# A third Strassen-type pair in the gate/up projection, and two groups of PSUM banks that change places

## The chip, the cores and the metric

The kernel runs on one core of a Trainium2 chip. The core has a matrix engine (TensorE, PE in the profile, with its weight loads as PEld), three engines for elementwise work (VectorE or DVE, ScalarE or ACT, GpSimd or POOL) and SyncE (SP), which issues most of the loads here. Matmuls write to PSUM, eight banks of 128 x 512 fp32 values; everything else lies in SBUF. The metric is the time of one execution on the device, in microseconds (us), the median of several runs.

## What is computed

One decoder layer on 256 tokens of width 2048, in fp32. The change touches the feed-forward part alone:

```python
ff = silu(u @ w_ffn_gate) * (u @ w_ffn_up)    # u: 256 x 2048, weights 2048 x 5632
h = h + ff @ w_ffn_down                       # 5632 x 2048
return rmsnorm(h, final_norm_w)
```

Ahead of it stand an input projection, a recurrent unit (RG-LRU), a retention unit with eight heads, and an output projection added to the residual `h`; `u` is the normalised `h`.

## The kernel before

**Products in three matmuls.** Every fp32 operand is split in two parts, a rounded high one and the rest as a low one. ScalarE casts the high part (line 101) and VectorE subtracts it from the operand (line 102). A product of a left block (128 x 128, the stationary operand) and a right block (128 x 512, the moving one) is then three matmuls: high by high, high by low, low by high (lines 667 to 669). All three add up in one PSUM bank.

**Quads.** Gate/up runs as 11 blocks (`NB`), each for 512 columns of gate and the same 512 of up. A block goes through eight quads. A quad covers 256 of the 2048 input features: the left side is a 2 x 2 arrangement of 128 x 128 blocks `a11` to `a22` (rows are the two halves of the tokens, columns the two halves of the features), and the right side a 2 x 2 arrangement of 128 x 512 blocks `b11` to `b22` (rows are the halves of the features, column 1 is gate, column 2 is up). The four outputs are `c11`, `c21` (gate, two halves of the tokens) and `c12`, `c22` (up).

**Eight or seven products.** A plain quad takes the eight products of `EIGHT`. A quad whose number is in `SUMMED` takes the seven of `SEVEN`, a Strassen-Winograd scheme: the right side needs the sums `t1` to `t4` (lines 628 to 632, VectorE), the left side the sums `s1` to `s4` (lines 532 to 535, made once for a pair, in the output projection before). Four of the seven products, `p1`, `p5`, `p6`, `p7`, are shared: they add up over all summed quads of a block in four banks of their own, and are read after the last one and combined into starting values of the outputs (`post`, lines 723 to 732). Before the change `SUMMED` holds 2 and 4. The down projection has its own list, `SUMMED_DOWN`, and uses the same `block` function.

**What a quad loads and cuts.** `Quad.load` is called for each half of a quad: one transfer of 512 KB into a slot of the pool `raw` (five slots of 128 x 1024), issued by SP (line 614). A plain quad splits each half into one slot each of `wh` and `wl` (pool `split`, four slots of either). A summed quad splits `b11` by itself, makes the sums in two further slots of `raw`, and then splits `t1` with `t2`, `t3` with `t4` and `b22` with `b21`, three slots of `wh` and `wl`.

**PSUM.** Two pools of four banks: `bank` (pool `pmm`) and `aux` (pool `paux`). In gate/up and down, the outputs `c11` to `c22` take `aux` and the shared products `p1` to `p7` take `bank` (line 663). `bank` also serves the transposes of the gated product (`turn`, lines 714 to 721), those of the residual in blocks 1 and 2 (`resid_tok`, line 579) and the two small matmuls of the norm (`norm2`, line 568).

**The end of a block.** With `c12` and `c22` complete, `post` adds the shared part (lines 733 to 736), and `gated` applies tanh on ScalarE and two multiplications on VectorE (lines 708 to 712). `turn(0)` and `turn(1)` transpose the result for the down projection, and ScalarE copies it out (line 721). They are put off with `defer(n, ...)`, which runs a function n program steps later; a step is one quad. `turn(0)` is put off by 2 and `turn(1)` by 3: behind the first and the second quad of the next block.

**Who sets the order.** The program is traced step by step, with loads three half-quads ahead. The order of each engine's instructions is then settled at build time by a planner, which goes by data, free slots and modelled durations, with earlier traced work first (`schedule_with_timeline_sim=True`, line 1060). So matmuls of a later product can stand ahead of earlier ones. On the chip each engine runs its list in order and waits where an operand or a slot isn't there. Only the end of the last down block is ordered by hand (line 683).

Of the kernel before, what the change touches and what calls it, by code (L numbers as in the profile page):

```python
# [28 lines left out]

SUMMED = (2, 4)
SUMMED_DOWN = (2, 5, 8, 11, 14)


# [1 line left out]
def tile_hymba_layer(ctx: ExitStack, tc: tile.TileContext, A: dict, out: bass.AP):  # L37
# [17 lines left out]
    def nm(s):  # L55
        counter[0] += 1
        return f"{s}_{counter[0]}"

    def act_tile(name, dt=F32):
        return apool.tile([P, 512], dt, tag="act", name=nm(name))  # L60
# [7 lines left out]
    def bank(name):  # L68
        return pmm.tile([P, 512], F32, tag="mm", name=nm(name))
# [10 lines left out]
    def xs(k):  # L80
        return xt[k // 2][:, (k % 2) * S : (k % 2) * S + S]
# [137 lines left out]
    def defer(steps, f):  # L219
        later.append([steps, f])  # L220
# [12 lines left out]
    def rsqrt_small(dst, var, scale, n):  # L233

        t0 = cpool.tile([P, n], F32, name=nm("rs0"))
        t1 = cpool.tile([P, n], F32, name=nm("rs1"))
        act.activation(out=t1, in_=var, func=AF.Sqrt, scale=scale, bias=eps_t)
        v.tensor_scalar(out=t0, in0=var, scalar1=scale, scalar2=EPS, op0=ALU.mult, op1=ALU.add)
        v.reciprocal(out=t1, in_=t1)

        v.tensor_tensor(out=t0, in0=t0, in1=t1, op=ALU.mult)
        v.tensor_tensor(out=t0, in0=t0, in1=t1, op=ALU.mult)
        v.tensor_scalar(out=t0, in0=t0, scalar1=-0.5, scalar2=1.5, op0=ALU.mult, op1=ALU.add)
        v.tensor_tensor(out=dst, in0=t0, in1=t1, op=ALU.mult)
# [300 lines left out]
    def out_post(f, ps):  # L545
# [10 lines left out]
        if f % 2:  # L556
            hh[f // 2] = Left(hf[0], f // 2 in SUMMED)
        sq = sumsq[:, :S] if f == 0 else act_tile("sq")[:, :S]
# [6 lines left out]

    def norm2():

        ps = bank("rms")
        for t in range(2):
            pe.matmul(ps[:, 2 * t : 2 * t + 2], sumsq[:, t * P : t * P + P], ones[:, 0:2], start=True, stop=True)  # L570
        rsqrt_small(r2_tok, ps[:, 0:4:2], 1.0 / D, 2)
        v.tensor_scalar(out=r2_half, in0=r2_tok, scalar1=0.5, scalar2=None, op0=ALU.mult)
        v.tensor_tensor(out=r2_sq, in0=r2_half, in1=r2_tok, op=ALU.mult)
# [2 lines left out]

    def resid_tok(cb):
        for t in range(2):
            ps = bank("ht")
            for i in range(4):  # L580
                pe.transpose(ps[:, i * P : i * P + P], xs(4 * cb + i)[:, t * P : t * P + P], ident)
            htok[(cb, t)] = xpool.tile([P, 512], F32, tag="xh", name=nm("htok"))
            act.copy(out=htok[(cb, t)], in_=ps)

# [5 lines left out]
    class Quad:  # L592
# [19 lines left out]
        def load(self, half):  # L612
# [20 lines left out]
            self.cut(("t3", "t4"), tb)  # L633
            self.cut(("b22", "b21"), r)

    EIGHT = (
        ("c11", "a11", "b11"), ("c11", "a12", "b21"), ("c21", "a21", "b11"), ("c21", "a22", "b21"),
        ("c12", "a11", "b12"), ("c12", "a12", "b22"), ("c22", "a21", "b12"), ("c22", "a22", "b22"),
# [6 lines left out]
    def block(quads, lefts, post, ps, tail=(), after=None, ordered=False):  # L645


        n = len(quads) - (2 if tail else 0)
        todo = [(i, c, a, b, 0, 512) for i, q in enumerate(quads[:n]) for c, a, b in (SEVEN if q.sums else EIGHT)]
        for c, c0, cw in tail:  # L650
            todo += [(n, c, a, b, c0, cw, i) for i in range(n, len(quads)) for o, a, b in EIGHT if o == c[:3]]
        firsts, lasts = {}, {}
        for m, (_, c, *_) in enumerate(todo):
            firsts.setdefault(c, m)
            lasts[c] = m
        at = [0]

        def step(i):
            def run():
                while at[0] < len(todo) and todo[at[0]][0] == i:  # L660
                    m, (_, c, a, b, c0, cw, *q) = at[0], todo[at[0]]
                    if firsts[c] == m:
                        ps[c] = (aux if c in ("c11", "c12", "c21", "c22") else bank)(c)
                    q = q[0] if q else i
                    (ah, al), (bh, bl) = lefts[q][a], (t[:, c0 : c0 + cw] for t in quads[q].parts[b])
                    p, last = ps[c][:, c0 : c0 + cw], lasts[c] == m
                    pe.matmul(p, ah, bh, start=firsts[c] == m, stop=False)  # L667
                    pe.matmul(p, ah, bl, start=False, stop=False)  # L668
                    pe.matmul(p, al, bh, start=False, stop=last)  # L669
                    if last:  # L670
                        post(c)
                    at[0] += 1
                if after:
                    after(i)

            return run

        for i in range(n):
            program.append(([quads[i]], step(i)))
        if tail:  # L680

            def end():
                with tc.manual_schedule(engines={nc.tensor.engine}) if ordered else ExitStack():
                    step(n)()

            program.append((quads[n:], end))

    def ffn_block(j):
        def after(i):
            if j == 0 and i == SUMMED[-1] + 1:  # L690
                norm2()
            if j in (1, 2) and i < 2:
                resid_tok(2 * j - 2 + i)
            if j == NB - 1 and i == 0:
                load_fw()

        ps = {}
        quads = [Quad(A["w_gu"][j * (KT // 2) + i], i in SUMMED) for i in range(KT // 2)]
        block(quads, hh, ffn_post(j, ps), ps, after=after)

    def ffn_post(j, ps):
        part = {}

        def other(c, name, a, b, op=ALU.subtract):
            part[c] = act_tile(name)
            v.tensor_tensor(out=part[c], in0=a, in1=b, op=op)

        def gated(t):
            g, u, th = part["c21" if t else "c11"], part["c22" if t else "c12"], act_tile("th")
            act.activation(out=th, in_=g, func=AF.Tanh, scale=r2_half[:, t : t + 1])  # L710
            v.scalar_tensor_tensor(out=g, in0=th, scalar=1.0, in1=g, op0=ALU.add, op1=ALU.mult)
            v.scalar_tensor_tensor(out=g, in0=u, scalar=r2_sq[:, t : t + 1], in1=g, op0=ALU.mult, op1=ALU.mult)

        def turn(b):
            pt = bank("ft")
            for c in range(2):
                for t, g in enumerate((part["c11"], part["c21"])):
                    o = c * S + t * P
                    pe.transpose(pt[:, o : o + P], g[:, (2 * b + c) * P : (2 * b + c) * P + P], ident)  # L719
            ff[2 * j + b] = act_tile("ff")  # L720
            act.copy(out=ff[2 * j + b], in_=pt)

        def post(c):
            if c == "p1":
                part["c11"] = act_tile("c11")
                act.copy(out=part["c11"], in_=ps[c])
            elif c == "p7":
                n = act_tile("n")
                v.tensor_tensor(out=n, in0=ps["p6"], in1=part["c11"], op=ALU.subtract)
                other("c12", "c12", n, ps["p5"])  # L730
                other("c21", "c21", n, ps["p7"])
                other("c22", "c22", part["c21"], ps["p5"])
            elif c in ("c11", "c12", "c22"):
                v.tensor_tensor(out=part[c], in0=ps[c], in1=part[c], op=ALU.add)
            elif c == "c21":
                v.tensor_tensor(out=part[c], in0=ps[c], in1=part[c], op=ALU.subtract)
            if c == "c12":
                gated(0)
            if c == "c22":
                gated(1)  # L740
                defer(2, lambda: turn(0))
                defer(3, lambda: turn(1))

        return post

# [3 lines left out]
    def load_fw():  # L749
        for c in range(4):  # L750
            fw[c] = late_tile("fw")
            nc.sync.dma_start(out=fw[c], in_=A["final_norm_w"][c * 512 : c * 512 + 512].partition_broadcast(P))
# [136 lines left out]
    for n in range(NLRU):  # L889

        def post(ps, n=n):
            defer(max(1, 4 - n), lambda: lru_in(n, ps))
            defer(max(9, 12 - n), lambda: lru_gate(n))
            if n == NLRU - 1:
                defer(10, lru_roots)
                for m in range(NLRU):
                    defer((12, 15, 18, 20, 22, 24, 26, 28)[m], lambda m=m: lru_scan(m))
# [54 lines left out]
    for step, (units, run) in enumerate(program):  # L952
        need += 2 * len(units)
        while done < min(len(loads), need + AHEAD):
            un, j = loads[done]
# [108 lines left out]
```

## Time and profile before

| | us |
|---|---|
| runs shown: median (lowest to highest) | 1105.15 (1104.84 to 1106.02) |
| the profiled execution | 1106.04 |
| its span, first to last instruction | 1103.3 |
| gate/up begins | 382.8 |
| gate/up blocks 5 to 10, each | 43.15 |

The granted clock of TensorE is 0.998 on the mean. In the rows of the profile a group is written as line, engine, operation, the tiles it writes and reads (out<-in), its shape and count; then the busy time in us, the mean duration of one in ns, and after the second bar the idle time of the engine just before these instructions, with what ended it. In a table of stretches the first number is the length, and then come each engine's busy time and instructions, the granted clock, the share of the DMA engines and GB/s. In the timeline a row is start, duration, engine, line, what it does, how many in a row were merged, and in brackets the idle time before it and its releaser. Matmul ends are modelled, so their starts are the better measure.

### The profile page before, as it was taken

Reading aid. Unit: us, or ns where it says so; the run is one execution under the profiler, and the core shown is the slowest. Engines: PE = TensorE matmul, PEld = TensorE weight load, DVE = VectorE, ACT = ScalarE, POOL = GpSimd, SP = SyncE. Lnnn points to the kernel's source line nnn. Section 1 sums busy time; section 2 is a strip of 40 time slices with the busy share of each in tenths; the row PEclk is TensorE's granted clock in tenths of the full one; section 3 lists DMA queues with packets and bytes.
Section 4 is the critical chain, followed back from the end, with each engine's and each line's share of the span. In section 5 each row is a group of like instructions: output and inputs, shape, how many; then the busy total and the mean of one; then the engine's idle time right before and its main releaser. Section 6 shows DMA issues by size and latency. Waiting matters only on the chain.

```text
span 1103.3 us, 14624 instructions
## 1 busy us (share of the span) xinstructions
PE 1092.4 (99%) x5328; PEld 920.5 (83%) x5328; DVE 885.3 (80%) x1249; ACT 622.1 (56%) x846; POOL 57.9 (5%) x64
## 2 busy tenths in 40 slices
PE   9999999999999999999999999999999999999996
PEld 7888888888888988888888888888888888888885
DVE  7798799978776787788787878877887999777874
ACT  7666644468665665554554545544545675554552
POOL 0602130000000000000000000000000000020001
PEclk9999999999999999999999999999999999999999
DMA  9765575554665465645746646556456465646562
GB/s 329 239 199 168 171 245 170 176 188 143 194 220 187 155 207 174 213 154 186 247 132 214 226 156 229 187 191 219 159 195 234 153 219 196 224 161 218 201 230 76
DMA packets 62215, 214.71 MB, mean 195 GB/s; under 512 B 7104, under 2 KB 7488, under 8 KB 62144
## 3 DMA queue, kind: packets, MB, share of 16 engines
q1 hardware_dynamic: 61344, 211.70, 57.6%
q0 software_dynamic: 512, 1.57, 0.5%
q8 instruction: 41, 0.67, 0.3%
q10 hardware_dynamic: 288, 0.52, 0.1%
q14 instruction: 30, 0.25, 0.1%
HBM read 211.67 MB, written 2.10 MB: 194 GB/s over the span
## 4 chain that ended last, share of the span: by engine, by line
PE 98%; DVE 0%; DMA 0%; SPq 0%; ACT 0%; issue 0%; DVEq 0%
PE c L667 18%; PE c L669 18%; PE c L668 18%; PE fm L140 16%; PE fm L141 8%; PE p L667 3%; PE p L668 3%; PE p L669 3%; PE tm L156 3%; PE tm L157 3%; PE tm L158 3%; PE ft L719 1%; DMA x<-in_x 0%; PE fm L147 0%; PE fm L145 0%; PE fm L146 0%
## 5 line engine op out<-in xcount | busy, mean ns | idle before, releaser
L102 DVE TENSOR_TENSOR wl<-raw,wh 128x1024 fp32r<-128x1024 f32 (+1 forms) x364 | 438.0, 1216 | 150.5 <-ACT wh L101 146.2
L101 ACT CAST wh<-raw 128x1024 fp32r<-128x1024 f32 (+1 forms) x364 | 371.3, 1032 | 273.7 <-PE c L669 136.9
L668 PE MATMUL c<-wl,ah 128*128 128x512 f32 x848 | 326.4, 391 | 0.0
L669 PE MATMUL c<-wh,al 128*128 128x512 f32 x848 | 325.7, 390 | 0.0
L667 PE MATMUL c<-wh,ah 128*128 128x512 f32 x848 | 286.4, 390 | 0.0
L668 PEld LDWEIGHTS c<-wl,ah 128*128 128x128 f32 x848 | 159.2, 188 | 32.8
L669 PEld LDWEIGHTS c<-wh,al 128*128 128x128 f32 x848 | 159.2, 188 | 32.7
L667 PEld LDWEIGHTS c<-wh,ah 128*128 128x128 f32 x848 | 159.1, 188 | 32.6
L140 PE MATMUL fm<-u,wh 128*128 128x512 f32 x512 | 180.1, 396 | 0.0
L141 PE MATMUL fm<-u,wl 128*128 128x256 f32 x512 | 143.9, 281 | 0.0
L101 ACT CAST wh<-sum 128x1024 fp32r<-128x1024 f32 x64 | 66.9, 1053 | 87.0 <-PE c L669 40.2
L140 PEld LDWEIGHTS fm<-u,wh 128*128 128x128 f32 x512 | 96.0, 188 | 22.1
L141 PEld LDWEIGHTS fm<-u,wl 128*128 128x128 f32 x512 | 96.7, 189 | 0.2
L102 DVE TENSOR_TENSOR wl<-sum,wh 128x1024 fp32r<-128x1024 f32 x64 | 77.1, 1224 | 3.1 <-ACT wh L101 2.4
L140 PE MATMUL fm<-y,wh 128*128 128x512 f32 x224 | 78.8, 397 | 0.0
L141 PE MATMUL fm<-y,wl 128*128 128x256 f32 x224 | 62.5, 281 | 0.0
L823 POOL TENSOR_TENSOR htok<-htok,fw 128x512 f32<-128x512 f32 (+1 forms) x7 | 10.9, 1574 | 904.8 <-ACT junk L821 904.8
L140 PEld LDWEIGHTS fm<-y,wh 128*128 128x128 f32 x224 | 41.9, 188 | 10.2
L158 PE MATMUL tm<-wh,u 128*128 128x512 f32 x128 | 48.8, 390 | 0.0
L157 PE MATMUL tm<-wl,u 128*128 128x512 f32 x128 | 48.7, 392 | 0.0
L156 PE MATMUL tm<-wh,u 128*128 128x512 f32 x128 | 46.0, 396 | 0.9 <-ACT u L277 0.9
L141 PEld LDWEIGHTS fm<-y,wl 128*128 128x128 f32 x224 | 42.3, 189 | 0.2
(246 smaller groups left out, 1231.0 us busy)
## 6 DMA issues: line engine op xcount, KB each, us to landing
raw<-in_w_gu SPq DMA_DIRECT2D x176, 512.0 KB, 5.1
raw<-in_w_down SPq DMA_DIRECT2D x88, 512.0 KB, 4.4
raw<-in_w_out SPq DMA_DIRECT2D x32, 512.0 KB, 3.7
raw<-in_w_lx SPq DMA_DIRECT2D x16, 512.0 KB, 4.7
raw<-in_w_k SPq DMA_DIRECT2D x16, 512.0 KB, 4.0
raw<-in_w_q SPq DMA_DIRECT2D x16, 512.0 KB, 4.2
raw<-in_w_rg SPq DMA_DIRECT2D x16, 512.0 KB, 3.7
raw<-in_w_lg SPq DMA_DIRECT2D x16, 512.0 KB, 4.0
```

Source lines behind the costliest of these rows:

```text
L101: act.copy(out=dst_h, in_=src)
L102: v.tensor_tensor(out=dst_l, in0=src, in1=dst_h.bitcast(F32), op=ALU.subtract)
L140: pe.matmul(ps, wh, hl, start=first, stop=False)
L141: pe.matmul(ps[:, :S], wl, hl[:, :S], start=False, stop=last)
L156: pe.matmul(ps, ah, wh, start=first, stop=False)
L157: pe.matmul(ps, ah, wl, start=False, stop=False)
L158: pe.matmul(ps, al, wh, start=False, stop=last)
L667: pe.matmul(p, ah, bh, start=firsts[c] == m, stop=False)
L668: pe.matmul(p, ah, bl, start=False, stop=False)
L669: pe.matmul(p, al, bh, start=False, stop=last)
L719: pe.transpose(pt[:, o : o + P], g[:, (2 * b + c) * P : (2 * b + c) * P + P], ident)
L823: pool.tensor_tensor(out=h, in0=h, in1=fw[cb][:, c0 : c0 + cw], op=ALU.mult)
```

## The change

`SUMMED` becomes 1, 3, 5. The two pools of banks stand in a list `rooms`, which is reversed at the first step of every block: outputs take `rooms[0]` and shared products `rooms[1]`, so what held the outputs in one block holds the shared products in the next. The first block has `aux` for the outputs, as before. The transposes of the gated product, those of the residual and the norm's matmuls take a bank of `rooms[1]`. `turn(1)` is put off by 2 steps like `turn(0)`. The norm is traced behind quad 5, as before (5 is now the last of `SUMMED`, and was the one behind it).

```diff
-SUMMED = (2, 4)
+SUMMED = (1, 3, 5)
...
     def norm2():
-        ps = bank("rms")
+        ps = rooms[1]("rms")
...
     def resid_tok(cb):
         for t in range(2):
-            ps = bank("ht")
+            ps = rooms[1]("ht")
...
+    rooms = [bank, aux]
+
     EIGHT = (
...
         def step(i):
             def run():
+                if i == 0:
+                    rooms.reverse()
                 while at[0] < len(todo) and todo[at[0]][0] == i:
...
-                        ps[c] = (aux if c in ("c11", "c12", "c21", "c22") else bank)(c)
+                        ps[c] = rooms[c[0] == "p"](c)
...
-            if j == 0 and i == SUMMED[-1] + 1:
+            if j == 0 and i == SUMMED[-1]:
                 norm2()
...
         def turn(b):
-            pt = bank("ft")
+            pt = rooms[1]("ft")
...
                 defer(2, lambda: turn(0))
-                defer(3, lambda: turn(1))
+                defer(2, lambda: turn(1))
```

## The prediction

> **What bounds the kernel now.** I read the page first, then the busy time by stretches of one gate/up block each, then the timeline of one block boundary.
>
> ```profile
> span 1103.3 us, 14624 instructions
> ...
> PE 1092.4 (99%) x5328; PEld 920.5 (83%) x5328; DVE 885.3 (80%) x1249; ACT 622.1 (56%) x846; POOL 57.9 (5%) x64
> ...
> PE 98%; DVE 0%; DMA 0%; SPq 0%; ACT 0%; issue 0%; DVEq 0%
> ```
>
> TensorE (PE) is busy for 99% of the span, and the chain that ended last is 98% matmuls. Busy matmuls overlap, so this alone does not prove that the array sets the pace; the stretches and the spacing of starts have to say it.
>
> ```profile
> core 0: us, PE busy (x) PEld busy (x) DVE busy (x) ACT busy (x) POOL busy (x), PEclk, DMA share, GB/s
> 563.00:606.15 43.15, 43.15 (x196) 35.67 (x195) 34.42 (x41) 22.62 (x25) 0.00 (x0) 1.00 0.61 195
> ...
> 778.75:821.90 43.15, 43.15 (x196) 35.66 (x195) 34.42 (x41) 22.40 (x25) 0.00 (x0) 1.00 0.57 195
> ```
>
> These are the first and the last of six consecutive gate/up blocks, each 43.15 us long. PE is never idle in them. VectorE (DVE) works 34.42 us of 43.15 (80%), ScalarE (ACT) 22.6 (52%).
>
> ```profile
> 600.78 0.39 PE L669 MATMUL c<-wh,al 128*128 128x512 f32 x1
> ...
> 607.81 0.39 PE L667 MATMUL c<-wh,ah 128*128 128x512 f32 x1
> ```
>
> In the timeline of PE these two matmuls are the first and the last of 32, across the end of a block, with no hole between them: 31 steps in 7.03 us, 0.2268 us each. A block has 2x7 + 6x8 = 62 products of three matmuls, 186 in all; 186 x 0.2268 = 42.18 us, and the 8 transposes take the other 0.97. So gate/up is paced by the number of matmuls alone, and the block boundary costs nothing today.
>
> **What the change removes.** A third summed pair turns eight products into seven once more in each of the 11 blocks: 3 x 0.2268 = 0.68 us a block, 7.48 us in all. A new block would be 42.47 us. That is the whole possible gain, as no wait of PE is left to be removed.
>
> By the Trainium skill (Perfetto Trace Analysis, Identifying the Most-Contended Engine) matmul busy time is a poor measure of TensorE's headroom, and the busy share of weight loads is a better one. Here that share is 35.67 / 43.15 = 83%, which would leave room on PE and put the gain in doubt; by that rule the sum could be 0 in place of 7.48. The even spacing of starts speaks for the count of matmuls, so the rule gets a small chance below.
>
> **What it adds on DVE and ACT.** Groups of one block, DVE first, then ACT:
>
> ```profile
> L102 DVE TENSOR_TENSOR wl<-raw,wh 128x1024 fp32r<-128x1024 f32 x15 | 18.1, 1223 | 6.6 <-ACT wh L101 6.6
> L102 DVE TENSOR_TENSOR wl<-sum,wh 128x1024 fp32r<-128x1024 f32 x4 | 4.8, 1225 | 0.1
> L628 DVE TENSOR_TENSOR sum<-raw 128x512 f32<-128x512 f32 x2 | 1.4, 687 | 2.1 <-DMA raw<-in_w_gu 2.1
> L102 DVE TENSOR_TENSOR bl<-raw,bh 128x512 fp32r<-128x512 f32 x2 | 1.4, 686 | 0.0
> ```
> ```profile
> L101 ACT CAST wh<-raw 128x1024 fp32r<-128x1024 f32 x14 | 14.6, 1054 | 11.2 <-PE c L669 9.1 <-PE p L669 1.2 <-DMA raw<-in_w_gu 0.9
> L101 ACT CAST bh<-raw 128x512 fp32r<-128x512 f32 x2 | 1.2, 613 | 0.4 <-DMA raw<-in_w_gu 0.4
> ```
>
> A plain quad costs DVE two 1024-wide subtractions. A summed one costs four 512-wide adds (lines 628 to 632), one 512-wide subtraction and three 1024-wide ones. Records of DVE overlap, so I count from start to start, in the timeline of the boundary:
>
> ```profile
> 596.85 2.36 DVE L102 TENSOR_TENSOR wl<-raw,wh 128x1024 fp32r<-128x1024 f32 x2 [3.53 <-ACT wh L101]
> 599.13 0.68 DVE L734 TENSOR_TENSOR c<-c,c 128x512 f32<-128x512 f32 x1
> ...
> 605.19 2.36 DVE L102 TENSOR_TENSOR wl<-raw,wh 128x1024 fp32r<-128x1024 f32 x2
> 607.46 0.75 DVE L712 SCALAR_TENSOR_TENSOR c<-c,r_sq,c 128x512 f32<-128x512 f32 x1
> 608.12 0.69 DVE L631 TENSOR_TENSOR sum<-raw,raw 128x512 f32<-128x512 f32 x1
> 608.73 0.69 DVE L632 TENSOR_TENSOR sum<-sum,raw 128x512 f32<-128x512 f32 x1
> 609.33 2.51 DVE L102 TENSOR_TENSOR wl<-sum,wh 128x1024 fp32r<-128x1024 f32 x2
> ...
> 615.46 0.69 DVE L628 TENSOR_TENSOR sum<-raw 128x512 f32<-128x512 f32 x1 [1.44 <-DMA raw<-in_w_gu]
> ...
> 620.74 2.36 DVE L102 TENSOR_TENSOR wl<-sum,wh 128x1024 fp32r<-128x1024 f32 x2
> ```
>
> A 512-wide step is 0.60 us (608.12 to 608.73), a 1024-wide one 1.135 (two from 605.19 to 607.46). The extra is 5 x 0.60 + 1.135 = 4.14 us of DVE a block, and 1.05 + 0.61 = 1.66 of ACT. DVE goes to 38.6 of 42.47 us (91%), ACT to 24.3. On the mean both still fit under PE, which is why I cost them at nothing there; that cover has 3.9 us of DVE left in a block, from 8.7.
>
> **Where the cover is thin.** The mean is not enough. The split weights have four 1024-wide slots: a plain quad holds two, a summed one three. The raw weights have five slots, and a summed quad takes two more for its sums. So DVE can't run far ahead, and the question is how late a summed quad's split is against the matmul that reads it.
>
> ```profile
> 608.04 0.38 PE L719 MATMUL ft<-ident,c 128*128 128x128 f32 x2
> 608.17 0.48 PE L667 MATMUL p<-bh,ah 128*128 128x512 f32 x1
> ...
> 614.64 0.40 PE L668 MATMUL p<-wl,sh 128*128 128x512 f32 x1
> ...
> 625.33 0.39 PE L668 MATMUL p<-wl,sh 128*128 128x512 f32 x1
> ```
>
> The low half of the first summed quad's t1 is ready at 609.33 + 1.23 = 610.56 and first read at 614.64: 4.08 us in hand. For the second it is 621.97 against 625.33: 3.36. A summed and a plain quad together take DVE 11.41 us from split to split, and PE 10.69, so 0.72 us of slack is lost in each such cycle. The change makes two cycles (1 to 3 to 5) of one, and it begins one quad nearer to the boundary, where DVE also has the eight steps from 599.13 to 607.46 that turn the last outputs into the gated product. Then PE comes 24 x 0.2268 = 5.44 us earlier, and DVE is relieved of one quad's two cuts, 2.27: the slack at quad 1 is 4.08 - 5.44 + 2.27 = 0.91 us, at quad 3 0.19, at quad 5 -0.53.
>
> So, if nothing else moves, PE waits 0.53 us a block; if the order written at build time uses the DVE idle time left (3.53 us before 596.85), it waits 0. That is the unknown, between 0 and 5.8 us in 11 blocks; below nothing is excluded, as PE has no wait to lose. I take 0.17 us a block, 1.9 in all, nearer to the rows, which show PE at work through the same pattern and taking a product of a later quad early (608.17) when its own is late. The first block carries the same risk, with the end of the output projection beside it, and is counted with the rest.
>
> **Edits at nothing.** Trading the groups of banks lets a block begin without the outputs of the last being read; PE waits for that nowhere now (31 even steps across the boundary), so 0. The second transposed half moves one step earlier, and both now take two of the four banks that quad 1's shared products want:
>
> ```profile
> 613.58 0.59 ACT L721 COPY ff<-ft 128x512 f32<-128x512 f32 x1 [0.82 <-PE ft L719]
> ```
>
> The first two products have banks and give 6 x 0.2268 = 1.36 us of cover; the two copies are 1.18 and queue on ACT behind casts that can wait for a slot. Between 0 and 1.2 us a block, I take 0 since PE can take other products. In blocks 1 and 2 two of the four residual transposes ask for a bank while four shared products hold that group; they slip behind quad 5, and nobody reads them before the down projection. The norm's small matmuls (line 568) stay behind quad 5, where in the first block the shared products now end too: they wait for the first bank that is read out, and their result is wanted only in quad 7. The extra sums of the left side come once:
>
> ```profile
> 345.00:382.80 37.80, 37.80 (x246) 34.28 (x245) 27.67 (x45) 21.99 (x37) 0.00 (x0) 1.00 0.57 181
> ```
> ```profile
> L532 DVE TENSOR_TENSOR s<-hf 128x128 f32<-128x128 f32 x1 | 0.3, 288 | 0.0
> ```
>
> Four such and one 512-wide step, under 2 us, in a stretch where DVE has 10 us free beside a PE that is never idle: 0. DMAs are as many and as large as before.
>
> **The sum.** The profiled execution took 1106.04 us, its span 1103.3; 1106.04 - 7.48 + 1.9 = 1100.46. It lies 0.89 above the median of the runs, so against the median: 1105.15 - 7.48 + 1.9 = 1099.6 us.
>
> **Rivals.** *DVE becomes the bound (slower).* Other blocks lose more in a cycle:
>
> ```profile
> 566.19 2.51 DVE L102 TENSOR_TENSOR wl<-sum,wh 128x1024 fp32r<-128x1024 f32 x2
> ...
> 572.97 0.69 DVE L628 TENSOR_TENSOR sum<-raw 128x512 f32<-128x512 f32 x1 [2.08 <-DMA raw<-in_w_gu]
> ...
> 578.25 2.36 DVE L102 TENSOR_TENSOR wl<-sum,wh 128x1024 fp32r<-128x1024 f32 x2
> ```
> ```profile
> 571.51 0.40 PE L668 MATMUL p<-wl,sh 128*128 128x512 f32 x1
> ...
> 582.19 0.39 PE L668 MATMUL p<-wl,sh 128*128 128x512 f32 x1
> ```
>
> Here DVE needs 12.06 us from split to split and PE 10.68, because the first add stands in DVE's queue 2.08 us for a weight that could be loaded only when the sums before it gave back their slots. Lost slack 1.38 a cycle; with two cycles 0.91 - 2.76 = -1.85 us a block, 20.4 in 11: 1105.15 - 7.48 + 20.4 = 1118. It decides from 0.68 us of waiting a block. Against it: the wait for a DMA shrinks as soon as DVE itself is late. Chance 0.16.
>
> A rule that would make this worse: the Trainium skill (TensorE: Matmul & The Clock Gate, Why this matters for your kernels) warns that idle gaps of more than about 3 us between matmuls drop the clock. The granted clock is 1.00 in every stretch quoted, and the waits above are under 2 us. I put 0.01 of the 0.16 on it; a gap of 3 us in each of 11 blocks gives 1105.15 - 7.48 + 33 = 1131 or more.
>
> *The gain is eaten (no difference).* Waits of 0.5 to 0.9 us a block, by the upper bound above and a little over; 0.68 gives exactly 1105. With it stands the case that the count of matmuls isn't the pace, which leaves 1105. Chance 0.12, 0.03 of it the latter.
>
> *Nothing waits.* 1105.15 - 7.48 = 1097.7, the lower end of the forecast.
>
> **How the numbers follow.** Forecast, with waits of 0 to 0.48 us a block: 0.72, time 1097.7 to 1102.9, likeliest 1099.6. The scatter of the runs is 0.3 below the median and 0.9 above, so the range begins at 1097.0. It goes up to 1109, which takes in the upper bounds and the mild part of the slower case; 0.13 is left above and some 0.05 below. About 0.2% (2.2 us) is what a measurement of this kernel can tell from no change: faster 0.72, same 0.12, slower 0.16.
>
> **What would show it.** Right: six blocks of 42.5 to 42.7 us, 99 matmuls fewer, line 628 33 times in gate/up, DVE near 38.6 us a block, idle PE under 0.3 us a block. Wrong: idle PE of over 0.6 us a block ahead of the p products of quad 5 or of quad 1, with a DVE split or an add waiting for a load as its releaser; or, for the trade of banks, PE waiting for the copy of the transposes ahead of the third and fourth shared product.

## The result and the profile after

| | before | after |
|---|---|---|
| median of six runs, us | 1105.21 | 1116.8 (1113.84 to 1122.8) |
| ratio, with its 95% interval | 1 | 1.0111 (1.0094 to 1.0129) |
| the profiled execution, us | 1106.04 | 1113.84 |

The changed kernel is slower by 1.1%, where faster was forecast, and outside the forecast's range of 1097 to 1109 us. The profiled execution is the fastest of the six, so the profile shows the loss somewhat small. The page of the changed kernel opens like this (span, busy times, the chain that ended last by engine):

```profile
span 1112.0 us, 14637 instructions
...
PE 1092.2 (98%) x5295; PEld 911.7 (82%) x5295; DVE 931.5 (84%) x1320; ACT 636.8 (57%) x869; POOL 58.4 (5%) x64
...
PE 65%; DVE 17%; DMA 12%; ACT 3%; issue 2%; SPq 0%; DVEq 0%; ACTq 0%
```

The work went as the change says: 5328 - 5295 = 33 matmuls fewer, three in each of 11 blocks. (The prediction's last part says 99. That is a slip in counting; its 7.48 us are 33 x 0.2268.) The busy line is of little help otherwise, as PE still reads 98%. The last line is the finding. Before, the chain was 98% PE. Now 29% of it is VectorE and transfers.

How long is a block now? These are stretches from one block's read of `p1` to the next one's, blocks 4 to 10, with the table's last row:

```profile
588.60:632.60 44.00, 43.07 (x192) 34.83 (x191) 38.37 (x47) 23.73 (x29) 0.00 (x0) 1.00 0.56 191
632.60:677.60 45.00, 43.40 (x192) 34.90 (x192) 38.54 (x47) 23.74 (x29) 0.00 (x0) 1.00 0.56 187
...
sum 265.00, PE 258.99 PEld 209.31 DVE 230.73 ACT 142.38 POOL 0.00; mean PE 43.16 PEld 34.89 DVE 38.45 ACT 23.73 POOL 0.00
```

VectorE's load is what was forecast (38.45 us a block, against 38.6) and the clock is full (1.00). But a block takes 265.00 / 6 = 44.17 us instead of 42.47. So 1.70 us a block is lost, where the forecast had 0.17 and its slower rival 1.85. The medians give nearly the same: (1116.8 - 1105.2 + 7.48) / 11 = 1.74. For the profiled execution as a whole the same sum is (1113.84 - 1106.04 + 7.48) / 11 = 1.39, so these six blocks lose more than its others. VectorE is idle for 44.17 - 38.45 = 5.7 us of a block. Its own work is not the bound.

What it waits for, and what PE waits for, is in the table of waits for the same six blocks (engine, line and tile, what it waited for; then us in total, times, longest):

```profile
DVE sum L629 <- DMA raw<-in_w_gu: 29.8, 12, 4.4
...
PEld ft L724 <- DVE c L717: 6.6, 6, 1.1
PEld c L673 <- DVE wl L102: 6.3, 12, 1.1
PE ft L724 <- DVE c L717: 4.0, 6, 0.7
```

and for six blocks of the kernel before:

```profile
DVE wl L102 <- ACT wh L101: 41.6, 25, 3.5
...
DVE sum L628 <- DMA raw<-in_w_gu: 10.4, 6, 2.4
```

Before, VectorE mostly waited for ScalarE's cast, that is, it had caught up with everything, and PE does not appear among the waiters. After, the wait has gone over to the first add of a summed quad (line 628 before, 629 now), which stands at the head of VectorE's list until its weight has landed: from 10.4 to 29.8 us. PE appears twice: at the transposes of the gated product (line 724, for the multiplication on line 717) and at plain products, for the low half of the weight.

The timeline of VectorE shows such a wait (start, duration, what; in brackets the idle time ahead and its releaser):

```profile
662.33 2.36 DVE L102 TENSOR_TENSOR wl<-sum,wh 128x1024 fp32r<-128x1024 f32 x2 [0.31 <-ACT wh L101]
664.61 1.22 DVE L102 TENSOR_TENSOR wl<-raw,wh 128x1024 fp32r<-128x1024 f32 x1
670.19 0.69 DVE L629 TENSOR_TENSOR sum<-raw 128x512 f32<-128x512 f32 x1 [4.36 <-DMA raw<-in_w_gu]
670.80 1.22 DVE L102 TENSOR_TENSOR wl<-raw,wh 128x1024 fp32r<-128x1024 f32 x1
```

and PE in the same microseconds, then at the transposes of the next boundary:

```profile
670.79 0.50 PE L672 MATMUL p<-bh,ah 128*128 128x512 f32 x1
672.07 0.50 PE L673 MATMUL c<-wl,ah 128*128 128x512 f32 x1 [0.78 <-DVE wl L102]
```
```profile
698.66 0.40 PE L672 MATMUL c<-wh,sh 128*128 128x512 f32 x1
699.72 0.44 PE L724 MATMUL ft<-ident,c 128*128 128x128 f32 x2 [0.65 <-DVE c L717]
```

The start of a matmul comes 1.28 us after the one before it in the first pair and 1.06 in the second, where 0.2268 is the pace. How the late load comes to hold up PE at 672.07 is in ScalarE's timeline:

```profile
666.42 1.05 ACT L101 CAST wh<-raw 128x1024 fp32r<-128x1024 f32 x1 [2.21 <-PE c L674]
```

This is the cast for the split that PE waits for. It was done at 667.47, but the split stands behind the add in VectorE's list, and began only at 670.80, when the add had had its load. So a load for a later quad holds up a split that PE wants sooner. The order of the list is part of the loss, not the lateness of the load alone.

The loads of that stretch, by tile (first and last issue, then the time from issue to landing):

```profile
L615 SPq DMA_DIRECT2D raw<-in_w_gu x4: 327/328/328, 660.3 to 664.7; - x4
...
DMA to landing us min/median/max: 3.3/5.1/6.6
```

The last two went out as the two pieces of the split from 662.33 ended and gave back the slots of the sums: one at 663.6, the other at 664.7 (662.33 + 2.36 = 664.69). The first of these two is the load that the add waits for. It took 6.5 us, and the add began at 670.19. The chain across the next boundary (start, duration, what) shows that this closes into a loop:

```profile
674.99 4.94 DMA raw<-in_w_gu
...
681.11 1.24 DVE wl L102
682.37 5.30 DMA raw<-in_w_gu
...
690.11 0.69 DVE sum L630
690.79 1.14 DVE wl L102
691.93 0.60 DVE sum L632
692.53 0.60 DVE sum L633
...
695.53 2.27 DVE wl L102 x2
697.79 1.20 DVE c L716 x2
699.00 0.67 DVE c L717
...
699.72 0.44 PE ft L724 x2
...
705.66 0.24 PE c L674
...
705.97 1.06 ACT wh L101
707.05 1.24 DVE wl L102
708.30 5.52 DMA raw<-in_w_gu
```

Each load starts within 0.03 us of the end of the split that frees its slot (681.11 + 1.24 = 682.35, then 682.37). When it lands, VectorE has a queue without a hole (690.11 to 699.67), in which the gated product stands behind the late splits, and the transposes wait for that. Then the chain runs over PE's matmuls from 699.72 to 705.90, which give back a slot of `wh`, over the cast that takes this slot, and over the next split, which frees the next slot of `raw`. Load, add, split, matmuls, cast, split, load: the time of a load is part of the round, and no engine has to be full for the round to set the pace.

### The profile page after: what moved, and what is told of

It reads as the page before. It is cut to its first block, busy times and chain, and to the rows that moved or that the text cites. A ratio compares the mean times of both kernels' runs of the same rounds, so it can differ in the third digit from the quotient of the medians.

```text
span 1112.0 us, 14637 instructions
## 1 busy us (share of the span) xinstructions
PE 1092.2 (98%) x5295; PEld 911.7 (82%) x5295; DVE 931.5 (84%) x1320; ACT 636.8 (57%) x869; POOL 58.4 (5%) x64
## 4 chain that ended last, share of the span: by engine, by line
PE 65%; DVE 17%; DMA 12%; ACT 3%; issue 2%; SPq 0%; DVEq 0%; ACTq 0%
PE fm L140 15%; DMA raw<-in_w_gu 11%; PE c L673 8%; PE c L674 8%; PE c L672 8%; DVE wl L102 8%; PE fm L141 8%; PE tm L156 3%; PE tm L157 3%; PE tm L158 3%; PE p L672 2%; PE p L674 2%; PE p L673 2%; ACT wh L101 2%; DVE c L739 2%
## 5 line engine op out<-in xcount | busy, mean ns | idle before, releaser
L102 DVE TENSOR_TENSOR wl<-raw,wh 128x1024 fp32r<-128x1024 f32 (+1 forms) x353 | 424.8, 1215 | 70.9 <-ACT wh L101 66.4
L673 PE MATMUL c<-wl,ah 128*128 128x512 f32 x782 | 303.8, 393 | 2.5 <-DVE wl L102 2.2
L674 PE MATMUL c<-wh,al 128*128 128x512 f32 x782 | 301.2, 390 | 0.0
L672 PE MATMUL c<-wh,ah 128*128 128x512 f32 x782 | 255.9, 391 | 1.1 <-ACT wh L101 1.1
L101 ACT CAST wh<-sum 128x1024 fp32r<-128x1024 f32 x86 | 89.0, 1052 | 98.7 <-DVE sum L630 35.0
L102 DVE TENSOR_TENSOR wl<-sum,wh 128x1024 fp32r<-128x1024 f32 x86 | 103.1, 1223 | 6.6 <-ACT wh L101 5.8
L629 DVE TENSOR_TENSOR sum<-raw 128x512 f32<-128x512 f32 x43 | 29.8, 692 | 56.6 <-DMA raw<-in_w_gu 49.9
L101 ACT CAST bh<-raw 128x512 fp32r<-128x512 f32 x51 | 31.4, 623 | 56.6 <-DMA raw<-in_w_gu 44.2
L673 PE MATMUL p<-wl,sh 128*128 128x512 f32 x129 | 50.2, 389 | 0.0
L674 PE MATMUL p<-wh,sl 128*128 128x512 f32 x129 | 50.2, 390 | 0.0
```

The source lines that it names most:

```text
L101: act.copy(out=dst_h, in_=src)
L102: v.tensor_tensor(out=dst_l, in0=src, in1=dst_h.bitcast(F32), op=ALU.subtract)
L629: v.tensor_tensor(out=t1, in0=b11, in1=b12, op=ALU.add)
```

## The experiments

Two theories stood at the outset. *Load loop*: the above, five slots of `raw` with sums and loads in them. *Transposes and banks*: the trade of groups, with both transposed halves early, makes PE wait for the gated product (the 6.6 us of line 724). A third reading, the plain sense of the prediction's rival, is *VectorE's work*: that 38.5 of 42.5 us is simply too tight, wherever the slots are. No run leaves out any part of the computation. Ratios are to the kernel before, run on the same chip (1105.2 to 1105.3 us).

**The change taken in two.** e1 has the trade of the banks and the earlier half, with `SUMMED = (2, 4)` kept. e2 has the third pair without the trade; `turn(1)` is put off by 2, since the shared products of quad 1 then want all four banks of `bank`.

```diff
-                        ps[c] = (aux if c in ("c11", "c12", "c21", "c22") else bank)(c)
+                        ps[c] = rooms[c[0] == "p"](c)
...
-                defer(3, lambda: turn(1))
+                defer(2, lambda: turn(1))
```
```diff
-SUMMED = (2, 4)
+SUMMED = (1, 3, 5)
...
-            if j == 0 and i == SUMMED[-1] + 1:
+            if j == 0 and i == SUMMED[-1]:
...
-                defer(3, lambda: turn(1))
+                defer(2, lambda: turn(1))
```

> The bank trade and the earlier second transposed half, with the two summed quads of before (2 and 4) and nothing more on VectorE. Load theory (the third summed quad's first add waits for a weight whose slot the sums hold): no change, 1104.5 to 1106. Transpose theory (TensorE waits at the transposes because both halves now stand behind the first quad, ahead of the finished gated product): 0.8 us a block stay, 1112 to 1115. Work theory (4.14 us more of VectorE a block are simply too much): no change, 1104.5 to 1106.

> The third summed pair (1, 3, 5) with both transposes one step earlier, but the shared products keep one group of banks and the outputs the other. If the trade of banks is worth something at this spacing, the next block's first products now wait until VectorE has read the last outputs: slower than the change, 1119 to 1128. If the trade is worth nothing, as priced in the prediction: like the change, 1114 to 1120.

e1: 1104.91 us, 0.9994 (0.9984 to 1.0003), its chain 98% PE as before. e2: 1118.23 us, 1.0113 (1.0074 to 1.0153), the loss of the whole change. So the trade and the earlier half cost nothing by themselves, and the loss came with the third pair. The waits of gate/up in e2 show where PE stands without the trade:

```profile
DVE sum L628 <- DMA raw<-in_w_gu: 36.5, 18, 3.0
...
PE c L667 <- DVE c L734: 11.3, 8, 1.7
```

PE has no wait at the transposes here; it waits for the outputs of the last block to be read out (line 734), because the next block's outputs want the same banks. The waiting place moved, and the time stayed. The line at which PE waits is not the cause.

**More slots.** e3 is the change with seven slots of `raw`; to make room, the pool of activations goes from 58 tiles to 55. e4 is the kernel before with the same edit, and e8 the kernel before with 55 tiles and five slots.

```diff
-    apool = ctx.enter_context(tc.tile_pool(name="acts", bufs=58))
+    apool = ctx.enter_context(tc.tile_pool(name="acts", bufs=55))
...
-    rpool = ctx.enter_context(tc.tile_pool(name="raw", bufs=5))
+    rpool = ctx.enter_context(tc.tile_pool(name="raw", bufs=7))
```

> The change with seven slots for raw weights in place of five (paid with three of the 58 activation tiles). Load theory: the wait of the sums' first add for a load falls from 5.0 us a block to under 1.5, and most of the loss goes, 1098 to 1106. Transpose theory: the waits at the transposes stay at 0.8 us a block, 1106 to 1110. Work theory: VectorE has as much to do as before, no change, 1113 to 1118.

> Control: the kernel before with seven slots for raw weights and 55 activation tiles. All theories: TensorE has no wait to lose, 1104 to 1106; a gain of over 1 us would mean that the slots help elsewhere (the input projection), and would have to be taken off what the seven slots bring in the change.

> Control for the seven slots: the kernel before with 55 activation tiles and five slots. If the three tiles given up are what cost the kernel before 5.5 us with seven slots: 1108 to 1112, with waits after gate/up's last block. If the two further loads in flight did it: 1104.5 to 1106.

e3: 1107.38 us, 1.0014 (1.0003 to 1.0026), just above what the load theory expected and within the 1106 to 1110 of the transpose theory. But PE has no wait at the transposes in gate/up, so it isn't the transposes. e4: 1110.88, 1.005 (1.0035 to 1.0065), where no change was expected. e8: 1105.49, 1.0002 (0.9992 to 1.0011). So the 55 tiles cost nothing, and the two further slots cost the kernel before 5.5 us, mostly in the down projection: more room lets the planner write another order. Against that control the three pairs are 3.5 us faster, and inside gate/up the forecast nearly holds. Stretches of e3 from `p1` to `p1`, blocks 5 to 10, and its waits over all of gate/up:

```profile
621.30:664.10 42.80, 42.75 (x193) 35.00 (x192) 38.59 (x48) 24.08 (x29) 0.00 (x0) 1.00 0.58 198
...
sum 213.70, PE 213.42 PEld 174.84 DVE 192.92 ACT 120.45 POOL 0.00; mean PE 42.68 PEld 34.97 DVE 38.58 ACT 24.09 POOL 0.00
```
```profile
DVE wl L102 <- ACT wh L101: 35.3, 36, 2.1
...
DVE sum L629 <- DMA raw<-in_w_gu: 4.7, 5, 2.0
```

VectorE does the same 38.58 us a block, and a block takes 213.70 / 5 = 42.74. That answers the third theory: 90% of VectorE fits under PE when the loads come in time.

**Room for one user alone.** In e5 the two sums get two slots of their own through blocks 0 to 9, in space that stands empty until block 10; the loads stay in the five of `raw`. e6 is the kernel before with that, and e7 the three pairs with that and without the trade. The diff below leaves out the function `sum_tile`, which takes a slot of the new pool while there is one, and the lines that close that pool in block 10.

```diff
-            ta, tb = (rpool.tile([P, 1024], F32, tag="raw", name=nm("sum")) for _ in range(2))
+            ta, tb = (sum_tile() for _ in range(2))
...
-        late.append(ctx.enter_context(tc.tile_pool(name="late", bufs=5)))
+        sums[1] = ctx.enter_context(ExitStack())
+        sums[0] = sums[1].enter_context(tc.tile_pool(name="sums", bufs=2))
```

> The change, with the right-hand sums of gate/up's first ten blocks in two slots of their own (in space that is free there), so that all five slots for raw weights serve loads; activation tiles 58 as before, nothing moved outside gate/up. Load theory: waits of the first add for a load under 1 us a block, waits at the transposes gone too since they came from a late VectorE, gate/up near 42.5 to 42.8 us a block, 1097 to 1101. Transpose theory: 0.6 us a block stay at the transposes, 1104 to 1107. Work theory: 1112 to 1118.

> Control: the kernel before, with the sums in the same two slots of their own. All theories: TensorE has no wait to lose in gate/up, 1104.5 to 1106.

> As the run with three summed quads, both transposes a step earlier and no trade of banks, now with the sums in two slots of their own. If the trade only moved the wait that a late VectorE causes (it showed as products waiting for line 734 without the trade, as transposes waiting for line 717 with it), both are gone here: 1097 to 1102. If the trade has a worth of its own at this spacing, TensorE still waits for the outputs to be read, 1103 to 1110.

e5: 1112.01 us, 1.0063 (1.0049 to 1.0077). e6: 1108.03, 1.0025 (1.0014 to 1.0035). e7: 1116.63, 1.0101 (1.0088 to 1.0115). The load theory had expected 1097 to 1101 of e5 and missed. The sums were only one of the two holders of the slots. The halves of a summed quad are the other: the first keeps its slot until `b11` is split and `t3` has read it, the second until its own split, the quad's last. The loads still came late: the adds of e5 wait 17.1 and 9.1 us for them in gate/up. e6 missed its "no change" too. The trade of the banks is worth something in this setting: 1116.63 against 1112.01.

In e9 the two loads of a summed quad get the two slots instead, and the sums stay in `raw`. e10 is the kernel before with that, and e15 is e9 with three such slots.

```diff
-            r = rpool.tile([P, 1024], F32, tag="raw", name=nm("raw"))
+            r = (extra[0] if self.sums and extra[0] else rpool).tile([P, 1024], F32, tag="raw", name=nm("raw"))
...
-        late.append(ctx.enter_context(tc.tile_pool(name="late", bufs=5)))
+        extra[1] = ctx.enter_context(ExitStack())
+        extra[0] = extra[1].enter_context(tc.tile_pool(name="extra", bufs=2))
```

> The change, where the two loads of a summed quad go to two slots of their own in the first ten gate/up blocks (free space, 58 activation tiles), and the five slots serve plain loads and the sums. Load theory, as the seven-slot run left it (what counts is how far ahead of the first add a summed quad's load can be issued): first adds wait under 1 us a block for loads, no wait at the transposes, gate/up near 42.7 us a block, 1097 to 1101. If only seven slots open to everything help, as the run with the sums apart could mean: 1108 to 1114.

> Control: the kernel before with the same two slots for the loads of its two summed quads. Load theory: TensorE has nothing to win, 1104 to 1106. If more room makes the build-time order worse, as in the control with the sums apart: 1107 to 1110.

> As the run with own slots, with three of them in place of two. If the remaining loss is still loads that come late: 1098 to 1101.5. If not: 1102 to 1105.

e9: 1103.29 us, 0.9987 (0.9978 to 0.9996), 13.5 us better than the change, but short of the load theory's 1097 to 1101. e10: 1105.69, 1.0003 (0.9994 to 1.0012), so the room alone does nothing for the kernel before. This pair tells the theories apart: the work of every engine, the trade and the place of the transposes in the program are those of the change, and what was altered is the point at which a summed quad's loads can go out (with what the planner makes of it). Stretches of e9, the first two of blocks 4 to 10 with the table's last row, then its waits over the same stretch:

```profile
588.00:630.50 42.50, 42.50 (x192) 35.04 (x191) 38.56 (x47) 23.93 (x28) 0.00 (x0) 1.00 0.60 200
630.50:673.00 42.50, 42.50 (x192) 35.02 (x192) 38.55 (x47) 23.84 (x28) 0.00 (x0) 1.00 0.62 198
...
sum 256.70, PE 256.41 PEld 210.31 DVE 231.33 ACT 142.82 POOL 0.00; mean PE 42.74 PEld 35.05 DVE 38.55 ACT 23.80 POOL 0.00
```
```profile
DVE sum L632 <- DMA raw<-in_w_gu: 18.0, 10, 2.9
...
DVE sum L631 <- DMA raw<-in_w_gu: 6.5, 7, 4.6
```

The two blocks shown are the forecast's, 42.50 us with PE never idle; the six take 256.70 / 6 = 42.78 on the mean, the last of them 43.40. Yet VectorE still waits 18.0 + 6.5 = 24.5 us for loads in the six, 4 us a block where under 1 was expected, against 29.8 in the change. That is about its free time, 42.78 - 38.55 = 4.2 us a block, spent in front of whatever comes last. A wait for a load on VectorE's list is therefore no proof of a loss; a wait of PE, or the chain, is.

e15: 1107.92 us, 1.0024 (1.0015 to 1.0034), worse than with two slots, and outside both expectations. Its adds wait only 7.9 us for loads in gate/up, but PE now waits for VectorE's splits:

```profile
DVE sum L632 <- DMA raw<-in_w_gu: 7.9, 10, 3.1
PEld c L675 <- DVE wl L102: 7.3, 8, 1.2
```

With the weights there earlier, the sums of a later quad seem to be put ahead of the splits that PE wants first. That is read off this list, and no run tested it alone.

**Another place for the summed quads.** e11 sums 1, 4, 6 and e12 sums 2, 4, 6 (there with `turn(1)` put off by 3 again); the norm stays behind quad 5.

```diff
-SUMMED = (1, 3, 5)
+SUMMED = (1, 4, 6)
```
```diff
-SUMMED = (1, 3, 5)
+SUMMED = (2, 4, 6)
...
-                defer(2, lambda: turn(1))
+                defer(3, lambda: turn(1))
```

> The change with quads 1, 4 and 6 summed in place of 1, 3 and 5 (five slots): as much work for every engine, but two plain quads between the first two summed ones, so more time for the second one's loads. Load theory: first-add waits fall from 5.0 to some 2 to 4 us a block, 1105 to 1112. If it is the nearness of quad 1 to the block's end that costs, or the work: 1113 to 1119.

> The change with quads 2, 4 and 6 summed and the second transposed half put off by 3 again (five slots): as dense as 1, 3, 5, but a quad farther from the last block's end, and the transposes as before the change. Load theory: the dense stretch is the same, first-add waits of 4 to 5 us a block, 1111 to 1118. If nearness to the boundary or the earlier transposes cost: 1099 to 1106.

e12: 1116.49 us, 1.0096 (1.0083 to 1.011), the same as the change. So taking away both the nearness of quad 1 to the boundary and the earlier half brings nothing back. e11: 1126.78, 1.0185 (1.0166 to 1.0203), outside both expectations, where the load theory had wider spacing help. Its chain runs through three loads within a block:

```profile
660.36 4.60 DMA raw<-in_w_gu
...
670.38 4.57 DMA raw<-in_w_gu
...
680.42 5.82 DMA raw<-in_w_gu
```

It looks like the same loop with one load more in the round. Why that order came out so was not separated from the planner's choices.

**The residual's transposes.** e13 is the change with one `resid_tok` in each of blocks 1 to 4 in place of two in each of blocks 1 and 2; e14 is e9 with that.

```diff
-            if j in (1, 2) and i < 2:
-                resid_tok(2 * j - 2 + i)
+            if 1 <= j <= 4 and i == 0:
+                resid_tok(j - 1)
```

> The change with five slots, but the residual's transposes stand behind the first quad of blocks 1 to 4, one column block each, so that none asks for a bank while the shared products hold that group. Load theory: that is not where the time went, 1113 to 1118. If transposes that wait for the bank cost a good part: 1105 to 1111.

> The two slots of their own for summed loads, and the residual's transposes spread over blocks 1 to 4. In the run with own slots the last six blocks took 42.5 to 42.9 us and the first five lost 6 us. If the residual's transposes cause that loss: 1097.5 to 1100. If it is the start, where VectorE comes out of the output projection late: 1102 to 1105.

e13: 1112.0 us, 1.0066 (1.0052 to 1.008), between the two expectations. Its interval and the change's do not meet: with these transposes spread, the change is some 4.8 us faster. That their waiting for a bank makes all of it is not shown. The two profiled executions differ by 2.0 us (spans of 1112.0 and 1110.0), and 1.3 of it lie in the last five stretches from `p1` to `p1` (221.0 and 219.7 us), where neither has such transposes. e14: 1102.93, 0.998 (0.9971 to 0.9989), the fastest version here and 0.2% faster than the kernel before, as expected if the residual's transposes are not what e9 still loses; against e9 it is 0.4 us, which the intervals don't tell apart. Its chain by engine:

```profile
PE 86%; DVE 6%; DMA 5%; issue 1%; ACT 1%; SPq 0%; DVEq 0%; ACTq 0%
```

## Why the prediction was wrong, step by step

**The pace of PE and the gain: right.** Where nothing waits, a block is 42.50 us (two of e9's six, which average 42.78) against 42.47 worked out, so three matmuls fewer a block are worth what was said. The Trainium skill's rule quoted in the prediction (Perfetto Trace Analysis, Identifying the Most-Contended Engine) does not decide here: weight loads are busy 35.04 / 42.50 = 82% in e9 and were 83% before, and the block still shortened by 0.65 us with the matmuls removed.

**VectorE's and ScalarE's extra work: right.** 38.45 and 23.73 us a block, against 38.6 and 24.3. The cover on the mean held as well (e3, e9).

**The wait: wrong, and this is the step that failed.** The prediction took 0.17 us a block, "nearer to the rows", with an upper bound of 0.53. Both came from the milder of the two cycles it had measured, 0.72 us of slack lost in each, and the other, 1.38, went to a rival with 0.16. The measured 1.70 is close to that rival's 1.85. In part this is luck: the rival had PE wait elsewhere, and the whole profiled execution gives 1.39. Two things were wrong in the choice. First, one cycle seen in one block is no better evidence than another cycle seen in another; the rows gave a spread of 0.72 to 1.38, and the bounds of the term had to cover it. Second, the reason against the rival, that "the wait for a DMA shrinks as soon as DVE itself is late", supposes that the load has its own time of departure. The chain shows that it leaves when VectorE gives back a slot. If VectorE is late, so is the load, and the wait stays. And the wait is not VectorE's alone: splits that are ready stand behind it, and PE waits for them (672.07). It grew from 15.6 us (line 628 in gate/up before) to 49.9 in the page's group after:

```profile
  DMA raw<-in_w_gu: 15.6, 9
```
```profile
L629 DVE TENSOR_TENSOR sum<-raw 128x512 f32<-128x512 f32 x43 | 29.8, 692 | 56.6 <-DMA raw<-in_w_gu 49.9
```

The 43 adds are 33 in gate/up and 10 in the down projection, 11 more than the 32 before, as the change says.

**The rival's name was half right.** "DVE becomes the bound" had the place (the first add, behind a load that needs the sums' slots) and about the price. But VectorE is idle for 5.7 us a block. What bounds is the round through slots and loads, and e9, which leaves VectorE's work alone, gets 13.5 us of the loss back. It also put the waits of PE ahead of the `p` products of quads 5 and 1; they stand ahead of plain products and, because the gated product queues behind late splits, ahead of the transposes.

**Trade of the banks and transposed halves at 0: right by themselves** (e1, 1104.91). In the company of three pairs the trade saves time if anything (e7 against e5).

**The residual's transposes at 0: probably wrong in the change**, which is 4.8 us faster with them spread (e13). "Nobody reads them" was true, but they can wait for a bank, with others behind them; that this is how they cost is argued, not shown. With the loads in time (e14 against e9) nothing measurable is left.

**The clock: no part in it.** The Trainium skill's warning of a lower clock after gaps of over 3 us (TensorE: Matmul & The Clock Gate, Why this matters for your kernels) is not tested here: the longest wait of PE's rows above is 1.7 us, and the granted clock is 1.00 in all stretches shown.

**What stays open.** The forecast without waits was 1097.7; e14 stands at 1102.9. In the table of PE's waits, e14 has these in gate/up up to block 5 (to 628.1 us), and none from there to the last block (to 841.2):

```profile
PE ft L729 <- DVE c L722: 0.7, 1, 0.7
PE p L675 <- DVE wl L102: 0.4, 1, 0.4
PE c L675 <- DVE wl L102: 0.2, 1, 0.2
```

That is 1.3 us. In the last block come 0.8 more, for casts of ScalarE. So 2.1 of the 5.2 us in between are found; where the rest lies, and what sets the order in the first blocks, was not found out. Nor was it settled why the planner's orders in e4, e11 and e15 are worse. A shorter load with the slots unchanged, the direct test of the load's share in the round, was not tried; nor was an order of VectorE's list with the ready splits ahead of the add, nor more slots of `wh` and `wl`, which also stand in the round. All runs that move the slots also let the planner write another order, so the two shares are not separated.

## What to carry to other kernels

Where an engine's input is loaded into a slot that the same engine frees, count the round (free, load, use, free) against the time of the work it must supply, besides each engine's own load; the DMA engines here were busy 56% of the time, VectorE 87% (38.45 of 44.17 us), and the round still set the pace. Look also at what stands behind a waiting instruction on its engine's list. When a bound on a wait comes from a few cycles in a trace, take the spread of the cycles as the range, and ask of any reason that says a wait will shrink what starts the thing waited for. And give spare room to the buffer that closes the round, with the kernel before as a control: two slots for the loads gained 13.5 us, the same two for the sums 4.8, a third one lost 4.6.

## What the hardware showed beside

Of the four loads of 512 KB shown above, issued within 4.4 us, the shortest took 3.3 us and the longest 6.6, so the time of a load in the round is not one number. The time also scatters more in the change (1113.84 to 1122.8) and in e2 (1112.31 to 1123.01) than in e1 (1104.01 to 1105.57). Whether the loads cause this was not tested; e5, whose loads come late too, stays within 1111.53 and 1113.87.
